# A hybrid decoder layer on one core: fewer vector steps, v's transpose in full products, gate rank in 16-bit halves, low rank products' low half with zeros, bonus sums beside the next key norm

## The chip, the cores and the metric

The kernel runs on one core of one Trainium2 chip. The metric is the device time of one execution in microseconds, the median over several runs. Engines are named as the profile names them: PE is TensorE (matrix products; PEld its loads of the stationary block), DVE is VectorE, ACT is ScalarE, POOL is GpSimd, and SP issues the DMAs. A matrix product `matmul(ps, lhsT, rhs)` holds `lhsT` stationary in the array and streams `rhs` through it; a product with fewer than 128 rows or columns uses a part of the array, and products on different parts can run at the same time. "64*128" in a profile row is such a part: 64 rows, 128 columns.

## The reference

The model is one layer over 4096 tokens of width 1024. Two head groups read the same normalised input, and one projection follows their gated outputs.

```python
h = _rmsnorm(x, norm_w);  u = (h @ w_in)
# gated linear attention: 4 heads, key 64, value 128, gate rank 16
log_a = log_sigmoid(glr @ gate_up + gate_bias) / 16
o = gla_chunked(q, k, v, log_a);  o = o * rsqrt(mean(o*o) + eps) * gla_norm_w
gla_out = o * silu(gg)
# RWKV-7: 8 heads of 64; mixed = shifted token mix of r, rk, rv, wl, al
w = -softplus(-(w0 + tanh(wl) @ w_up)) - 0.5;  decay = exp(-exp(w))
a = sigmoid(a0 + al @ a_up)
kk = normalise(rk * k_k);  rk = rk * (1 + (a - 1) * k_a)
y = rwkv7_scan(r, decay, rk, rv, kk, a)     # S = S(diag(w) - kk^T(a kk)) + v^T k;  y = S r
y = (y - mean(y)) * rsqrt(var(y) + eps) * ln_w + ln_b
bonus = sum(r * rk * r_k) * rv
rwkv_out = (y + bonus) * silu(rg)
out = rmsnorm(x + concat(gla_out, rwkv_out) @ w_out)
```

## The kernel before, in words

Features lie on the 128 partitions and tokens along the free dimension. The tokens are taken in 8 blocks of 512 (`TB`); the recurrent parts work in chunks of 64 tokens for RWKV (`C`, 8 chunks a block) and 128 for the gated attention. A **unit** is one block of one pair of RWKV heads: 4 pairs x 8 blocks = 32 units, numbered u. Two heads of 64 fill the 128 partitions; `lo` and `hi` are their halves.

The large projections are done in 16-bit halves: weights and inputs are split into a high and a low float16 part, and three products (high-high, high-low, low-high) are summed. These are the rows `bank<-x,wr`, `bank<-x,wg`, `bank<-x,wo` and `bank<-wg,x`. The small stages use 32-bit products, of which the profile counts two instructions each.

The work is written as generators, the streams: `stream_x` (input and its norm), `stream_w` (splitting the weights, once, and the setup), `stream_a` (per unit `rwkv_ab`: projections, decay, key norm, the products inside a chunk, the triangular inverse, v), `stream_i` (`rwkv_i`: joins the 32x32 inverses into 64x64 ones), `stream_c` (`rwkv_c`: the chain over the chunks, spawning `rwkv_d`, the group norm, bonus and gate), `stream_p` and `stream_g` (the gated attention) and `stream_o` (output projection). While they run, nothing is issued: each operation is recorded with a cost from `cost` (line 312) and its dependencies. Then `forward` and `backward` (line 234 on) plan the order of all instructions on every engine, as a list plan by how late each may start, and the instructions are issued in that order. So all instructions carry line 368, and groups are told apart by tile names. A changed operation, or a changed cost, lets the plan set another order anywhere.

What the change touches:

- `newton` (620) computes a reciprocal square root of 128x128 sums on VectorE: a first guess by integer arithmetic (a shift into `nt`, then a subtraction into `ny`) and two iterations. It serves the key norm (`a`), the group norm of RWKV (`c`) and the other norms (`g`).
- `stat_mm` (637) sums over the features of each head with four products on column groups of the array; `bcast` (641) writes the rows to DRAM and reads them back broadcast, three DMAs on SP.
- `lora_mm` (772) computes decay and a from rank 64: a product of 128 rows with `uh` (high part, against the high and low halves of the input) and one of 64 rows with `ul` (low part).
- `rwkv_ab` (780): `rn` is the key norm; at the end of a unit the bonus sums are made from `r`, which by then holds r·rk·r_k: `stat_mm(pst, bones, r)`, a copy to `brow`, `bcast`, and a product with v into `bv`. Then v is transposed into `sv`, 16 products of 64x64 with `c64`, which also takes the mean over the head from v. `De`, `Do`, `Nb` (`de`, `do`, `nb`) hold the operands of two units in turn; unit u writes them when the chain of unit u-2 is done.
- `rwkv_i` (911): `Ta` is a transpose, `Vs` the copied first product, and a second product gives the missing block of the inverse.
- `rwkv_c` (935): per chunk a product into `ch`, a copy to `us`, a product, two copies to `sv`, a product, and a scaled sum with `psd` on VectorE gives the next state. `y` collects the output.
- `rwkv_d` (977): square, sums, root, broadcast, then the affine norm, the gate `tg` and the maximum for the 16-bit split.
- `gla_lr` (1002) and `gla_pair` (1061): the gate's 16 features, in four partial sums, and the gate itself.
- `setup` (1266): prepares gate and low rank weights once, early in the run.

## Time and profile before

| | |
|---|---|
| median of 3 runs | 2419.3 us (2418.5 to 2422.08) |
| the profiled execution | 2425.58 us, span 2423.8 us |
| TensorE busy | 2301.9 us, 95% of the span |
| VectorE busy | 1691.6 us, 70% |
| ScalarE busy | 1219.0 us, 50% |
| GpSimd busy | 851.4 us, 35% |
| TensorE clock granted, mean | 0.982 |
| instructions | 54428 |

In a group's row, "x64 | 18.2, 386 | 0.0" means 64 instructions, 18.2 us of busy time together, 386 ns from start to end of one, and no idle time before them; since products overlap, the time that one of them costs is the distance to the next start, which the timeline shows. A timeline row is start, length, engine, operation, out<-in, array part, shape, count, and in brackets the idle time ahead of it with what ended that. A row of waits is: who waited, for whom, us in total, how often, the longest. The table of stretches has for each the busy time of every engine, the granted clock, and the DMA share.

### The profile page before, as it was taken

The page shows a single profiled execution, that of the slowest core. Times are in us where ns is not written, and L with a number is a line of the kernel's source. Part 1 is how long each engine was busy: PE and PEld are TensorE (multiplying, and loading weights), DVE is VectorE, ACT ScalarE, POOL GpSimd, SP SyncE. Part 2 cuts the span into 40 slices and gives each one's busy share as a digit, 9 for nine tenths or more (in the row PEclk, how much of TensorE's full clock was granted, in tenths as well). Part 3 has the DMA queues.
Part 4 walks back from the last instruction along what each step waited for, and adds up shares of the span by engine and source line. Part 5 has one row for each costly group of instructions (what it writes and reads, how often), then busy time and mean ns, then how long its engine had stood idle before and what let it go on. Part 6 is the DMA issues. An engine that isn't in the chain of part 4 may idle for free.

```text
span 2423.8 us, 54428 instructions
## 1 busy us (share of the span) xinstructions
PE 2301.9 (95%) x20710; PEld 1344.5 (55%) x20710; DVE 1691.6 (70%) x3866; ACT 1219.0 (50%) x3123; POOL 851.4 (35%) x2217
## 2 busy tenths in 40 slices
PE   7899999999999999999999999999999998999986
PEld 3555565455555656545564555645565564654643
DVE  7877877568675776676675687666867577666755
ACT  7576565455454555444644545455445455534342
POOL 4442234434323533315334243343334353331300
PEclk9898999999999999999999999999999999999987
DMA  6675545355334543455424553345533454344431
GB/s 196 205 229 184 160 145 172 110 170 151 95 102 129 169 126 97 112 145 168 112 80 122 171 151 103 98 124 162 151 94 98 130 182 116 104 109 116 137 91 58
DMA packets 275387, 325.54 MB, mean 134 GB/s; under 512 B 131652, under 2 KB 132788, under 8 KB 275124
## 3 DMA queue, kind: packets, MB, share of 16 engines
q1 hardware_dynamic: 275124, 322.06, 46.0%
q8 instruction: 162, 2.65, 0.5%
q14 instruction: 101, 0.83, 0.1%
HBM read 276.90 MB, written 45.05 MB: 133 GB/s over the span
## 4 chain that ended last, share of the span: by engine, by line
PE 63%; DVE 22%; DMA 6%; ACT 5%; issue 2%; SPq 1%; POOL 1%; DVEq 0%; ACTq 0%; POOLq 0%
PE bank L368 56%; PE ch L368 6%; DVE nta L368 2%; PE y L368 2%; DVE bk L368 2%; DVE Nb L368 2%; DVE De L368 1%; DVE Do L368 1%; DVE mgg L368 1%; DVE mgr L368 1%; DMA bv<-bcdb 1%; DVE gbc L368 1%; SPq L368 1%; DVE cy L368 1%; DVE sv L368 1%
## 5 line engine op out<-in xcount | busy, mean ns | idle before, releaser
L368 PE MATMUL bank<-x,wr 128*128 128x512 f16 x3264 | 811.3, 382 | 13.2 <-DVE De L368 5.7
L368 POOL TENSOR_TENSOR tm<-Tc,f 128x60 f32<-128x60 f32 (+24 forms) x961 | 338.5, 352 | 661.7 <-DMA f<-nd 405.5
L368 PEld LDWEIGHTS <-wr 128*128 128x128 f16 x3264 | 309.1, 100 | 319.2 <-issue 32.4
L368 PE MATMUL bank<-x,wg 128*128 128x512 f16 x1536 | 388.8, 380 | 5.4 <-DMA wg<-wdr 4.4
L368 POOL TENSOR_TENSOR Tc<-Tc,tm 128x60 f32<-128x60 f32 (+24 forms) x961 | 342.3, 356 | 73.2
L368 PE MATMUL bank<-x,wo 128*128 128x512 f16 x1488 | 364.0, 385 | 0.7 <-DVE nva L368 0.5
L368 DVE SCALAR_TENSOR_TENSOR sv<-ch,PC,psd 64x64 f32<-64x64 f32 x448 | 126.2, 282 | 214.5 <-PE ch L368 205.9
L368 POOL TENSOR_TENSOR xacc<-xacc,xr 128x512 f32<-128x512 f32 x98 | 131.8, 1345 | 374.0 <-ACT xr L368 211.5
L368 ACT ACTIVATE psd<-sv,PC 64x64 f32<-64x64 f32 x512 | 171.6, 342 | 122.3 <-DVE sv L368 115.4
L368 PEld LDWEIGHTS <-wg 128*128 128x128 f16 x1536 | 143.8, 99 | 152.1 <-issue 9.6
L368 PEld LDWEIGHTS <-wo 128*128 128x128 f16 x1488 | 143.0, 101 | 143.4 <-issue 9.3
L368 PEld LDWEIGHTS <-x 128*128 128x128 f16 x3120 | 189.8, 99 | 33.1 <-issue 13.4
L368 PE MATMUL bank<-wg,x 128*128 128x128 f16 x3072 | 206.2, 220 | 1.7 <-DMA wg<-wdr 1.7
L368 ACT COPY sv<-ch 64x64 f32<-64x64 f32 x512 | 104.6, 204 | 100.2 <-PE ch L368 93.1
L368 ACT ACTIVATE sa<-bank,mu_s 128x512 f32<-128x512 f32 x104 | 71.5, 687 | 137.0 <-PE bank L368 135.7
L368 POOL MEMSET Tc<- 32x8 f32 (+1 forms) x160 | 23.6, 148 | 318.2 <-DMA td<-Tc 303.5
L368 PEld LDWEIGHTS ch<-us,Nb 128*128 128x128 f32 x512 | 87.2, 191 | 57.2 <-ACT us L368 42.7
L368 ACT COPY us<-ch 128x64 f32<-128x64 f32 x256 | 53.3, 208 | 125.0 <-PE ch L368 122.4
L368 PEld LDWEIGHTS ch<-sv,bk 128*128 128x128 f32 x512 | 89.4, 191 | 48.1 <-ACT sv L368 32.7
L368 PE MATMUL ch<-sv,bk 128*128 128x128 f32 x512 | 106.8, 291 | 5.6 <-ACT sv L368 5.6
L368 PE MATMUL ch<-us,Nb 128*128 128x64 f32 x512 | 95.6, 269 | 11.5 <-ACT us L368 9.1
L368 PEld LDWEIGHTS ch<-sv,De 128*64 128x64 f32 x512 | 49.3, 135 | 98.9 <-issue 42.6
(327 smaller groups left out, 4115.4 us busy)
## 6 DMA issues: line engine op xcount, KB each, us to landing
wr<-wdr SPq DMA_DIRECT2D x256, 256.0 KB
wg<-wdr SPq DMA_DIRECT2D x184, 256.0 KB
xr<-in_xT_dram SPq DMA_DIRECT2D x176, 256.0 KB
wo<-wdr SPq DMA_DIRECT2D x128, 256.0 KB
f<-nd SPq DMA_DIRECT2D x128, 128.0 KB
x<-in_wt_dram SPq DMA_DIRECT2D x29, 512.0 KB
wdr<-wo SPq DMA_DIRECT2D x25, 512.0 KB
out_dram<-mgg SPq DMA_DIRECT2D x33, 256.0 KB
```

The costliest lines, as they stand in the source:

```text
L368: put(t0, self.name, d, lag, cols, tiles, tab, outs, ins, lambda: f(*a, **kw))
```

## The change

- `newton`: the shift and the subtraction become one step, a product with -0.5 and a sum on the integer view.
- `lora_mm`: `ul` becomes two tiles of 128 rows, of which the other 64 are zero; the low product now uses all 128 rows.
- The bonus sums of a unit with p = 0, 1 or 2 are put down in a list and made in the next unit, in the second quarter of the bank of that unit's key norm sums; its copy, broadcast and product with v follow the key norm's broadcast. A unit with p = 3 does them itself, where they stood. `rwkv_d` waits until the unit's bonus has been recorded. The copy to `brow` now also applies the gate's scale.
- The affine step of `rwkv_d` with its scale is folded into the neighbouring steps (`lnh`, made at setup).
- v's transpose: 4 products of 128x128x128 with a block diagonal `c64` and 4 copies, instead of 16 products and 2 copies.
- `rwkv_i`: the first product writes 64 rows, with 32 that are not used, and one copy takes all 128.
- `rwkv_c`: one `psd` step over both heads and both halves instead of two; `us` and `psd` have one buffer instead of two; the square of y is taken from the accumulator before the copy.
- The gate: the 16 features are computed twice, side by side (`wgs` columns 16 to 31); one copy becomes the float16 high part and the other the low part, and the 16-row weights are laid out as two float16 tiles. Two 16-bit products take the place of one 32-bit product.
- `cost` gets other values for some vector operations.

```diff
@@ cost
+            if op == "copy_predicated":
+                runs = 0.09
+            elif n == 256 and o.shape[0] != 128:
+                runs += 0.04 if op == "transpose" else 0.09
+            elif op == "tensor_scalar" and few > 1:
+                runs = 0.06
@@ newton
-        V.tensor_scalar(t.bitcast(I32), v.bitcast(I32), 1, None, ALU.logical_shift_right)
-        V.tensor_scalar(y.bitcast(I32), t.bitcast(I32), -1.0, float(0x5F1FFFF9), ALU.mult, ALU.add)
+        V.tensor_scalar(y.bitcast(I32), v.bitcast(I32), -0.5, float(0x5F1FFFF9), ALU.mult, ALU.add)
@@ lora_mm
-        q = slice(64 * i, 64 * i + 64)
         T.matmul(ps, lhsT=uh[i][:, cs_], rhs=LR[0][i], start=True, stop=False)
-        T.matmul(ps, lhsT=ul[q, cs_], rhs=LR[0][i][q], start=False, stop=True)
+        T.matmul(ps, lhsT=ul[i][:, cs_], rhs=LR[0][i], start=False, stop=True)
@@ rwkv_ab
         pst = yield from need("r")
         stat_mm(pst, bones, rn)
+        late = bonus.pop() if bonus else None
+        if late:
+            stat_mm(pst[:, P:2 * P], bones, late[1])
         bcast(newton(pst[:, 0:P], None, None, 1e-24, "a"), 2, rn, "a")
+        if late:
+            add_bonus(pst[:, P:2 * P], *late)
...
-        yield after(r)
-        pst = yield from need("r")
-        stat_mm(pst, bones, r)
-        brow = sb(rt, [P, P], F32, "brow", 1)
-        S.copy(brow, pst[:, 0:P])
         bv = tA("bv", 2)
-        bcast(brow, 2, bv, "b")
-        V.tensor_tensor(bv, bv, v, ALU.mult)
-        rel("r")
+        bonus.append((u, r, v, bv, hinv[:, i:i + 1]))
+        if p == 3:
+            yield after(r)
+            pst = yield from need("r")
+            stat_mm(pst, bones, r)
+            add_bonus(pst[:, 0:P], *bonus.pop())
+            rel("r")
...
-        for c in range(NC):
-            t_ = slice(C * c, C * c + C)
-            T.matmul(pv[64:128, c, :], lhsT=v[0:64, t_], rhs=c64[0:64, :], start=True, stop=True)
-            T.matmul(pv[0:64, c, :], lhsT=v[64:128, t_], rhs=c64[64:128, :], start=True, stop=True)
-        S.copy(sv[64:128, :, 0, :], pv[64:128])
-        S.copy(sv[0:64, :, 1, :], pv[0:64])
+        for c in range(4):
+            T.matmul(pv[:, c], lhsT=v[:, P * c:P * c + P], rhs=c64, start=True, stop=True)
+        for k, q in enumerate((lo, hi)):
+            for e, o in enumerate((hi, lo)):
+                S.copy(sv[o, k::2, e, :], pv[q, :, e, :])
+    def add_bonus(rows, u, r, v, bv, iv):
+        brow = sb(rt, [P, P], F32, "brow", 1)
+        S.activation(brow, rows, AF.Copy, scale=iv)
+        bcast(brow, 2, bv, "b")
+        V.tensor_tensor(bv, bv, v, ALU.mult)
+        bonuses.add(u)
@@ rwkv_i
-                T.matmul(pl[q0 + 32:q0 + 64, 0, c, :], lhsT=nb[q0:q0 + 32, c, q0 + 32:q0 + 64], rhs=Ta[q0:q0 + 32, c, :],
+                T.matmul(pl[q0:q0 + 64, 0, c, :], lhsT=nb[q0:q0 + 32, c, q0:q0 + 64], rhs=Ta[q0:q0 + 32, c, :],
                          start=True, stop=True)
-        for q0 in (0, 64):
-            V.tensor_copy(Vs[q0 + 32:q0 + 64], pl[q0 + 32:q0 + 64, 0])
+        V.tensor_copy(Vs, pl[:, 0])
@@ rwkv_c
-            us = sb(rt, [P, 64], F32, "us", 2)
+            us = sb(rt, [P, 64], F32, "us")
-            psd = sb(rt, [P, 64], F32, "psd", 2)
-            for q_, d_, e in dd:
-                S.activation(psd[q_], sv[q_, c, e, :], AF.Copy, scale=PC[q_, c])
+            psd = sb(rt, [P, 2, 64], F32, "psd")
+            S.activation(psd, sv[:, c], AF.Copy, scale=PC[:, c])
...
+        S.activation(rs, py.rearrange("p c t -> p (c t)"), AF.Square)
         S.copy(y, py.rearrange("p c t -> p (c t)"))
-        S.activation(rs, y, AF.Square)
@@ rwkv_d
-        V.scalar_tensor_tensor(y, y, pkt[:, PK_LW + p:PK_LW + p + 1], bv, ALU.mult, ALU.add)
-        V.tensor_scalar(y, y, pkt[:, PK_LB + p:PK_LB + p + 1], hinv[:, i:i + 1], ALU.add, ALU.mult)
+        V.scalar_tensor_tensor(y, y, lnh[:, p:p + 1], bv, ALU.mult, ALU.add)
-        V.tensor_tensor(mgt[4 + p], y, tg, ALU.mult)
+        V.scalar_tensor_tensor(mgt[4 + p], y, lnh[:, 4 + p:5 + p], tg, ALU.add, ALU.mult)
@@ gla_lr
-        glr = sb(rt, [P, TB], F32, "glr")
-        S.activation(glr, pr, AF.Copy, scale=invs[:, NWT:NWT + 1])
+        glr = sb(rt, [P, TB], F16, "glr")
+        S.activation(glr, pr, AF.Copy, scale=1.0 / GUP)
+        S.activation(glr, glr, AF.Copy, scale=gus[:, 2:3])
+        V.scalar_tensor_tensor(glr, pr, 1.0 / GUP, glr, ALU.mult, ALU.add)
@@ gla_pair
-        T.matmul(pz, lhsT=gupt[:, P * j:P * j + P], rhs=glr, start=True, stop=True)
+        for i in range(2):
+            T.matmul(pz, lhsT=guw[:, i, P * j:P * j + P], rhs=glr, start=i == 0, stop=i == 1)
@@ setup
-        G.memset(wgs, 0.0)
         split(raw, scl[:, NWT:NWT + 1], wgs[:, 0, :, 0:16], wgs[:, 1, :, 0:16])
-        G.memset(gupt, 0.0)
-        for g in range(4):
-            D.dma_start(gupt[32 * g:32 * g + 16, :], gup)
+        G.tensor_copy(wgs[:, :, :, 16:32], wgs[:, :, :, 0:16])
+        gr = sb(rt, [P, 1024], F32, "f4", 1)[:, 0:256]
+        for g in range(8):
+            D.dma_start(gr[16 * g:16 * g + 16], gup)
...
+        yield from absmax_scale(gr, gus[:, 3:4], gus[:, 4:5], "W")
+        S.activation(guw[:, 0], gr, AF.Copy, scale=gus[:, 3:4])
+        V.scalar_tensor_tensor(guw[:, 1], gr, gus[:, 3:4], guw[:, 0], ALU.mult, ALU.subtract)
+        V.tensor_scalar_mul(guw[:, 1], guw[:, 1], gus[:, 1:2])
...
-        D.dma_start(c64, ck[:, CK_C64:CK_C64 + 64])
+        for q in (slice(0, 64), slice(64, 128)):
+            D.dma_start(c64[q, q], ck[q, CK_C64:CK_C64 + 64])
```

More of the change, by code (lines that the diff above doesn't have):

```diff
@@ L47 @@
 NC = TB // C
+GUP = 2.0 ** 19
 DECAY = math.exp(-0.5)
@@ L453, in hymba_kernel @@
     uh = [sb(one, [P, 512], F16, f"uh{i}") for i in range(2)]
-    ul = sb(one, [P, 512], F16, "ul")
+    ul = [sb(one, [P, 512], F16, f"ul{i}") for i in range(2)]
+    for t in ul:
+        G.memset(t, 0.0)
     usc = sb(one, [P, 8], F32, "usc")
-    gupt = sb(one, [P, 256], F32, "gupt")
+    guw = sb(one, [P, 2, 256], F16, "guw")
+    gus = sb(one, [P, 8], F32, "gus")
+    gbz = sb(one, [P, 2], F32, "gbz")
     half_p = sb(one, [P, 12], F32, "half_p")
@@ L579, in split_w @@
                 V.tensor_tensor(gnh[:, h:h + 1], hinv[:, i:i + 1], pkt[:, PK_GN:PK_GN + 1], ALU.mult)
+            else:
+                for j in range(i - W_RG, 8, 4):
+                    V.tensor_tensor(lnh[:, j:j + 1], hinv[:, i:i + 1], pkt[:, PK_LW + j:PK_LW + j + 1], ALU.mult)
         if n < ND:
@@ L977, in rwkv_d @@
     def rwkv_d(p, b, mgt, y, rs, bv, tg):
+        u = 4 * b + p
+        if u not in bonuses:
+            yield lambda: u in bonuses
         yield after(rs)
```

32 lines of the change are left out of this document (21 added, 11 removed).

## The prediction

> **What bounds the kernel now.** I read the page's first two parts and its chain, then who TensorE waits for, then busy time by stretch.
>
> ```profile
> span 2423.8 us, 54428 instructions
> PE 2301.9 (95%) x20710; PEld 1344.5 (55%) x20710; DVE 1691.6 (70%) x3866; ACT 1219.0 (50%) x3123; POOL 851.4 (35%) x2217
> PE 63%; DVE 22%; DMA 6%; ACT 5%; issue 2%; SPq 1%; POOL 1%; DVEq 0%; ACTq 0%; POOLq 0%
> ```
>
> ```profile
> PE bank L368 <- DVE bk L368: 15.5, 10, 6.0
> PE ch L368 <- DVE sv L368: 9.7, 17, 2.9
> ```
>
> ```profile
> core 0: us, PE busy (x) PEld busy (x) DVE busy (x) ACT busy (x) POOL busy (x), PEclk, DMA share, GB/s
> 0.00:30.00 30.00, 15.64 (x95) 7.53 (x96) 20.65 (x70) 18.03 (x28) 15.39 (x34) 1.00 0.75 239
> 200.00:2200.00 2000.00, 1944.23 (x17784) 1139.19 (x17784) 1384.16 (x3057) 1002.49 (x2635) 744.18 (x1965) 0.99 0.46 131
> 2350.00:2400.00 50.00, 39.85 (x286) 21.50 (x283) 27.61 (x72) 14.87 (x48) 0.00 (x0) 0.91 0.22 64
> ```
>
> TensorE is the bound: it idles 2423.8 - 2301.9 = 122 us, and only 2000 - 1944 = 56 us of that lie in the long middle. The rest is the start and the tail. No one waits much: the worst releaser costs 15.5 us. So an edit is worth what it takes from TensorE's own time, and an edit on VectorE or ScalarE only what it takes from those 122 us. I therefore price TensorE first, by start-to-next-start in the timeline, because matmul durations overlap.
>
> **v's transpose.** 16 products 64x64 a unit (two instructions each) become 4 of 128x128x128, 8 instructions.
>
> ```profile
> 1166.16 1.15 PE L368 MATMUL bank<-c,v 64*64 64x64 f32 x32
> 1167.24 0.49 PE L368 MATMUL ch<-sv,bk 128*128 128x128 f32 x2
> ...
> 1148.95 1.05 PE L368 MATMUL bank<-SC,vt 128*128 128x128 f32 x8
> 1149.84 0.59 PE L368 MATMUL bank<-x,wr 128*128 128x512 f16 x2
> ```
>
> Old: 1167.24 - 1166.16 = 1.08 us. New: eight instructions of exactly the new shape take 1149.84 - 1148.95 = 0.89 us. So 0.19 saved, and another 0.10 for the change of array form (next fence) where the old group stood alone between full products, which the timeline shows for 10 of 32 units: 32 x 0.19 + 10 x 0.10 = 7.1 us. Bounds: 0 (the new group pays an entry of its own) to 9.
>
> A rule speaks against this edit and the next. The Trainium skill, page "TensorEngine Tiling (Array Packing)", section "Theoretical Speedup", gives tiling up to 2x where a dimension is 64 or less, which is what both edits give up; by that rule this edit would double its 1.08 us, adding 35 us over 32 units. The rows above contradict it for 32-bit products: 0.89 against 1.08.
>
> **Low half of the low rank products.** 64 products go from 64 to 128 rows.
>
> ```profile
> 1027.28 0.38 PE L368 MATMUL bank<-lr,uh 128*128 128x512 f16 x1
> 1027.59 0.39 PE L368 MATMUL bank<-lr,ul 64*128 64x512 f16 x1
> 1027.91 0.39 PE L368 MATMUL bank<-x,wg 128*128 128x512 f16 x1
> ...
> 1189.11 0.39 PE L368 MATMUL bank<-lr,ul 64*128 64x512 f16 x2
> 1189.42 0.27 PE L368 MATMUL ch<-sv,De 128*64 128x64 f32 x1
> ...
> 715.95 2.12 PE L368 MATMUL bank<-x,wr 128*128 128x512 f16 x9
> 717.90 0.27 PE L368 MATMUL ch<-sv,bk 128*128 128x128 f32 x1
> ```
>
> A full product in a stream takes 1.95/9 = 0.217 us. The lone 64-row one takes 0.31 us before it starts and 0.32 until the next, so each form change costs 0.10 us: 0.42 against 0.217. But two that follow each other share the array: 0.31 us for the pair at 1189.11, against 0.43 in full form. The timeline has 30 single and 17 pairs; 18 singles and 5 pairs stand alone. 18 x 0.20 + 12 x 0.10 - 12 x 0.11 - 5 x 0.02 = 3.4 us saved. Bounds: 0 to 7.
>
> **Gate rank.** One 32-bit product becomes two 16-bit ones, 16 times.
>
> ```profile
> 1064.20 1.02 PE L368 MATMUL bank<-glr,gupt 128*128 128x512 f32 x2
> 1065.06 0.39 PE L368 MATMUL ch<-sv,bk 128*128 128x128 f32 x2
> ```
>
> 0.86 us against 2 x 0.217: 16 x 0.43 = 6.9 us saved, bounds 6 to 8. It adds per block one ScalarE pass and one VectorE pass over 128x512 (0.59 and 0.76 us by the cy and bv rows of the last fence); the gate's tile is only needed in a later stage, and TensorE has other projections until then. Without that cover it is 8 x 1.35 = 11 us.
>
> **Bonus sums** go beside the next key norm in 24 of 32 units.
>
> ```profile
> 1165.80 0.42 PE L368 MATMUL bank<-r,bones 128*32 128x128 f32 x8
> ...
> 1042.12 0.43 PE L368 MATMUL bank<-rn,bones 128*32 128x128 f32 x8
> 1042.37 0.40 PE L368 MATMUL bank<-crs,bones 128*32 128x128 f32 x8
> ...
> 1189.81 0.43 PE L368 MATMUL bank<-rn,bones 128*32 128x128 f32 x8
> ...
> 1267.58 0.43 PE L368 MATMUL bank<-crs,bones 128*32 128x128 f32 x8
> ```
>
> Alone it takes 1166.16 - 1165.80 = 0.36 us (plus 0.10 where it stands between full products); right behind another sum of the same form the next one starts after 0.25. So 0.16 on the mean: 24 x 0.16 = 3.8 us, bounds 2 to 6. The move carries a ScalarE copy, one DMA out, two broadcast DMAs on SP and a VectorE product past the inverse's gathers and the weight loads on SP. For unit 15 it moves from 1165.8 to 1189.8, and its user (the product after the norm at 1267.6) comes 78 us later, so it costs nothing. Without that cover the VectorE product would wait in order for its broadcast: 28.8 us of such waits stand in the profile already (last fence).
>
> **The inverse's first product** writes 64 rows instead of 32, so the stationary block has 64 columns.
>
> ```profile
> 1055.81 0.69 PE L368 MATMUL bank<-Ta,Nb 32*32 32x32 f32 x32
> 1056.43 3.41 PE L368 MATMUL bank<-x,wo 128*128 128x512 f16 x15
> ...
> 1004.12 0.33 PE L368 MATMUL ch<-us,Nb 128*128 128x64 f32 x2
> 1004.28 1.24 PE L368 MATMUL bank<-x,wo 128*128 128x512 f16 x5
> ...
> 1009.08 0.22 PE L368 MATMUL y<-De,sv 128*64 128x64 f32 x1
> 1009.14 0.22 PE L368 MATMUL y<-De,sv 128*64 128x64 f32 x1
> ```
>
> Now 0.62 us. The streamed columns stay 32, so it could stay at 0.62 (lower bound, 0). But a block wider than what is streamed is not free: us times Nb, 128 stationary and 64 streamed columns, takes 0.16 us for two instructions, where 64 and 64 repeat after 0.06. If the second waits for its load, 0.16 - 0.06 = 0.10 us load 128 columns, 0.053 load 64; on two row tiles at once that is 0.027 an instruction, 32 x 0.027 + 0.10 = 0.96 us. The nearest upper row is v's 64x64 group, 1.08. I take 0.97, since the load row matches the new ratio of two to one: +0.35 x 32 = **+11 us**, bounds 0 to 15.
>
> The Trainium skill, page "TensorE: Matmul & The Clock Gate", section "LDWEIGHTS (loading the stationary operand)", says the load takes columns/1.2 ns whatever the rows; 64 columns would be an estimated 53 ns, the same as from the row here.
>
> **VectorE and ScalarE.**
>
> ```profile
> L368 DVE TENSOR_SCALAR nta<-nva 128x128 int32<-128x128 int32 x96 | 25.8, 269 | 1.9
> L368 DVE TENSOR_SCALAR cy<-cy,pkt,hinv 128x512 f32<-128x512 f32 x32 | 17.4, 543 | 0.6
> L368 DVE COPY Vs<-bank 32x256 f32<-32x256 f32 x64 | 27.1, 423 | 8.4 <-PE bank L368 7.3
> L368 DVE TENSOR_TENSOR bv<-bv,v 128x512 f32<-128x512 f32 x32 | 24.4, 762 | 29.0 <-DMA bv<-bcdb 28.8
> L368 ACT ACTIVATE psd<-sv,PC 64x64 f32<-64x64 f32 x512 | 171.6, 342 | 122.3 <-DVE sv L368 115.4
> L368 ACT ACTIVATE Gst<-gt,nm 128x128 f32<-128x128 f32 x16 | 6.4, 399 | 3.4 <-DVE gt L368 3.1
> L368 ACT COPY cy<-y 128x512 f32<-128x512 f32 x32 | 18.7, 585 | 49.3 <-PE y L368 49.1
> ```
>
> Gone are the shift of the square root (25.8), the second affine step of the RWKV output (17.4) and half the copies of Vs (13.5); added about 10 (the gate, the setup). VectorE loses some 46 us. On ScalarE 512 pieces of 0.342 become 256 of about 0.40 (the 128x128 row): -69 us, with some +15 for four copies of v instead of two, the gate and the scaled bonus row. That is 3% and 4% of these engines. I value it by the idle time it can shorten: of the middle's 56 us I take an eighth, -7, bounds 0 to -25. The single buffers of us and psd cost nothing: each next one needs a state that is written after the last reader of the old.
>
> In the tail nothing covers these steps, so they count in full: one step of two roots (0.27 each), the affine step 0.54, and the copy of y, behind which the square no longer waits, 0.59 less some 0.1 for reading the accumulator: -1.6. The square holds that accumulator about 0.7 us longer; the next state chain starts some 10 us after, which hides it. At the start the setup gains a maximum, its four scale steps, and two weight halves: some 10 small steps in line (0.15 to 0.4 us each), 2 to 4 us, while TensorE has other projections; I take +2, bounds 0 to +6.
>
> **Sum**: -7.1 - 3.4 - 6.9 - 3.8 + 11 = -10.2 on TensorE; -7 - 1.6 + 2 = -6.6 of idle time: -17. The profiled execution took 2425.6 us (span 2423.8 and 1.8 around it), 6.3 above the median of the runs, 2419.3. So 2408.6 profiled, **2402** as a median, 0.7% faster. A measurement tells 0.2%, 4.8 us, from no change.
>
> **The rivals.** *A, the wide block is free* (0.62 stays): for it, the streamed columns are unchanged and 32x32 repeats after 0.017 an instruction; against it, the us row. 2402 - 11 = 2391; with VectorE's idle bound 2375. *B, waits don't follow*: each unit's inverse passes through DMAs and POOL before its state chain, which nothing here shortens; TensorE then waits for what it filled before, and half the TensorE gain goes with all of the idle gain: 2419 - 5 + 2 = 2416, no measurable change. For it: after the first wait row, TensorE waits for bk and De, which that loop feeds. Against it: the loop contains the state chain, which gets shorter too. *C, slower: the wide block's two row tiles do not load side by side.* Then 32 x 0.053 + 0.10 = 1.80 us against 0.62, +38 us over 32 units instead of +11: 2429. It decides against the change from +28 us, that is from 1.5 us a group. For it: a 64-column block spans both halves' column tiles, which no row shows with 32 rows. Against it: the 64x64 rows, 1.08 for 32, do overlap.
>
> **How the numbers follow.** Forecast 0.55, A 0.18, B 0.15, C 0.12. Forecast's own range 2390 to 2412. Faster: 0.55 + 0.18 and a third of B's spread, 0.05, = 0.78; no change 0.11 (B's rest, some of C's low end); slower 0.11. The range that holds 8 in 10 leaves out C's upper and A's lower part: 2380 to 2422.
>
> **What would show it.** In the timeline after: v's products as 8 instructions in about 0.89 us; no 64-row product with ul; the gate's pair in 0.43; the bonus sum 0.25 behind a key norm; the group writing from Ta at 0.97 (0.62 would be A, 1.8 C). TensorE's busy sum should fall by about 10 us and its idle by 7; VectorE to about 1645, ScalarE to about 1165. I am wrong if busy falls and idle grows by as much (B), or if TensorE's busy rises.

## The result

The changed kernel takes 2381.3 us (median of four runs, 2378.8 to 2382.2) against 2419.6 us for the kernel before beside it: a ratio of 0.984, 95% interval 0.982 to 0.986, so 38 us or 1.6% faster. The forecast was 2402 us, 0.7% faster. The sign was right and the time lies inside the range of 2380 to 2422, at its very edge, but below the forecast's own 2390 to 2412; the gain is 2.2 times the one forecast, and rival B's and C's times, 2416 and 2429, are clearly missed. Rival A's, 2391 down to 2375, bracket the time, but not by A's cause, as the rows below show.

### The profile page after: what moved, and what is told of

The parts are those of the page before. It is cut to its first block, busy times and chain, and to the rows that moved or that the text cites. A ratio compares the mean times of both kernels' runs of the same rounds, so it can differ in the third digit from the quotient of the medians.

```text
span 2377.1 us, 52750 instructions
## 1 busy us (share of the span) xinstructions
PE 2276.7 (96%) x19944; PEld 1350.5 (57%) x19944; DVE 1659.1 (70%) x3737; ACT 1158.3 (49%) x2940; POOL 870.0 (37%) x2219
## 5 line engine op out<-in xcount | busy, mean ns | idle before, releaser
L375 POOL TENSOR_TENSOR Tc<-Tc,tm 128x60 f32<-128x60 f32 (+24 forms) x961 | 359.9, 375 | 74.0
L375 PE MATMUL bank<-wg,x 128*128 128x128 f16 x3072 | 200.6, 221 | 5.1 <-DMA wg<-wdr 5.1
L375 ACT ACTIVATE psd<-sv,PC 128x128 f32<-128x128 f32 x256 | 102.2, 399 | 192.4 <-DVE sv L375 166.3
```

Source lines behind the costliest of these rows:

```text
L375: put(t0, self.name, d, lag, cols, tiles, tab, outs, ins, lambda: f(*a, **kw))
```

## The profile after, beside the one before

The first two lines of the page of the kernel after:

```profile
span 2377.1 us, 52750 instructions
PE 2276.7 (96%) x19944; PEld 1350.5 (57%) x19944; DVE 1659.1 (70%) x3737; ACT 1158.3 (49%) x2940; POOL 870.0 (37%) x2219
```

The span fell by 46.7 us (the profiled execution of before was one of its slower ones, 6.3 us above the median, so this is 8 more than the medians tell). TensorE is busy 25.2 us less and idle 2377.1 - 2276.7 = 100.4 us instead of 121.9: 21.5 less, where 6.6 were forecast. VectorE lost 32 us, ScalarE 61.

To see where, busy time by stage: start, middle, end. The columns are those of the table by stretch in the prediction (the stretch, its length, busy time of PE, PEld, DVE, ACT and POOL, the granted clock, DMA). First the kernel before, whose middle is shown there:

```profile
0.00:200.00 200.00, 166.94 (x1264) 95.67 (x1264) 157.85 (x443) 132.90 (x260) 80.60 (x183) 0.95 0.68 210
2200.00:2423.80 223.80, 190.69 (x1665) 109.65 (x1662) 149.54 (x369) 83.62 (x230) 26.59 (x69) 0.90 0.35 99
```

The same of the kernel after:

```profile
0.00:200.00 200.00, 163.56 (x1142) 91.15 (x1144) 152.69 (x439) 127.77 (x247) 82.70 (x180) 0.94 0.65 205
200.00:2200.00 2000.00, 1956.41 (x17402) 1164.94 (x17404) 1385.65 (x2992) 964.95 (x2513) 762.03 (x1972) 0.99 0.46 133
2200.00:2377.10 177.10, 156.72 (x1404) 94.44 (x1404) 120.74 (x307) 65.60 (x182) 25.28 (x67) 0.95 0.36 108
```

TensorE's idle time by stage, length less busy: start 33.1 to 36.4 us (+3.4; +2 forecast), middle 55.8 to 43.6 (-12.2; -7 forecast), end 33.1 to 20.4 (-12.7; -1.6 forecast). And the clock: the end was run at 0.90 of full speed before and at 0.95 after. I call (1 - granted clock) x length the time lost to the clock, an upper bound of it since an idle TensorE loses nothing. At the end it goes from 223.8 x 0.10 = 22 us to 177.1 x 0.05 = 9. Over the whole span, with the mean granted clock of 0.982 before and 0.986 after, it is 43.6 and 33.3: 10 us that the prediction did not price at all. What is left of the busy time, TensorE's work at full clock, went from 2301.9 - 43.6 = 2258 to 2276.7 - 33.3 = 2243: -15, where -10.2 was forecast. So **the 46.7 us are 15 of work, 10 of clock and 21.5 of idle time.** Counted only over the time in which TensorE is busy, the clock loss is 31.1 us before and 23.1 after, and the split reads 17, 8 and 21.5.

At the end the last units of RWKV come sooner after each other. The sums for the norm of units 30 and 31 on TensorE, before and then after, from the timeline (start, duration, instruction):

```profile
2352.42 0.43 PE L368 MATMUL bank<-crs,bones 128*32 128x128 f32 x8
2386.10 0.42 PE L368 MATMUL bank<-crs,bones 128*32 128x128 f32 x8
```

```profile
2322.88 0.43 PE L375 MATMUL bank<-crs,bones 128*32 128x128 f32 x8
2342.65 0.43 PE L375 MATMUL bank<-crs,bones 128*32 128x128 f32 x8
```

Unit 31 follows unit 30 after 33.7 us before and 19.8 after, and behind it remain 38 and 34 us. So of the 46.7 us, 29.5 had been won by unit 30, 13.9 are won between the two units and 3.3 behind them.

**The terms on TensorE.** The timeline of after, stand-alone groups and what follows them:

```profile
150.88 1.05 PE L375 MATMUL bank<-c,v 128*128 128x128 f32 x8
151.77 4.48 PE L375 MATMUL bank<-x,wg 128*128 128x512 f16 x20
...
249.42 0.43 PE L375 MATMUL bank<-rn,bones 128*32 128x128 f32 x8
249.67 0.40 PE L375 MATMUL bank<-r,bones 128*32 128x128 f32 x8
...
280.30 0.59 PE L375 MATMUL bank<-glr,guw 128*128 128x512 f16 x2
280.73 1.24 PE L375 MATMUL bank<-x,wg 128*128 128x512 f16 x5
...
291.18 1.12 PE L375 MATMUL bank<-Ta,Nb 32*64 32x32 f32 x32
292.24 1.04 PE L375 MATMUL bank<-x,wg 128*128 128x512 f16 x4
```

By start to next start: v's transpose 0.89 us (0.89 forecast), a bonus sum 0.25 behind a key norm (0.25), the gate's pair 0.43 (0.43), the inverse's wide product 1.06 (0.97; 0.62 before). Summed over all their rows of the timeline, less idle time before the next: v's transpose 35.6 to 31.7 us (-3.9), the two halves of the low rank products 30.5 to 28.7 (-1.8), the gate 14.6 to 7.3 (-7.3), bonus and key norm sums 22.9 to 19.4 (-3.5), the wide product 21.9 to 36.2 (+14.3). The group rows of the two profiles agree on the two largest:

```profile
L368 PE MATMUL bank<-Ta,Nb 32*32 32x32 f32 x1024 | 24.2, 194 | 2.7 <-DVE De L368 1.4 <-DVE Ta L368 1.3
L368 PE MATMUL bank<-glr,gupt 128*128 128x512 f32 x32 | 16.9, 610 | 0.4 <-DVE mgr L368 0.3 <-ACT glr L368 0.2
```

```profile
L375 PE MATMUL bank<-Ta,Nb 32*64 32x32 f32 x1024 | 38.8, 221 | 2.5 <-DVE Ta L375 2.5
L375 PE MATMUL bank<-glr,guw 128*128 128x512 f16 x32 | 9.7, 379 | 0.6 <-ACT ta L375 0.4 <-DVE glr L375 0.2
```

These terms make -2 alone, so most of the 15 us does not lie in the changed groups' own rows. One place that fits are the rows next to them: the array changes its form 1049 times instead of 1207, and at the 0.10 us that the prediction read for a change, 158 fewer would be up to 16 us. This is an estimate; no run isolates it. The work of one and the same set of TensorE instructions also moves with their order: in the nine kernels below that have the 20710 of before it lies between 2252 and 2266 us.

**The start.** The maximum of the second low rank matrix on VectorE, and the key norm sum of the first unit, before and after:

```profile
26.91 0.69 DVE L368 TENSOR_REDUCE amW<-glr 128x1 f32<-128x512 f32 x1
44.82 0.42 PE L368 MATMUL bank<-rn,bones 128*32 128x128 f32 x8
```

```profile
39.42 0.68 DVE L375 TENSOR_REDUCE amW<-rgs 128x1 f32<-128x512 f32 x1
53.50 0.43 PE L375 MATMUL bank<-rn,bones 128*32 128x128 f32 x8
```

The gate's preparation stands ahead of that matrix and delays it by 12.5 us and the first unit by 8.7. TensorE's idle time grew by only 3.4 there, since it had projections to do.

## The experiments

Two theories were put against each other. **Matrix theory**, that of the prediction: TensorE is the bound, an edit is worth what it takes from TensorE, and VectorE and ScalarE steps are worth a small share. **Vector theory**: TensorE's work is laid around chains of small VectorE and ScalarE steps; shorter chains shrink idle time and raise the clock, while matrix work alone is mostly turned into waiting. A third suspect came up on the way: the order of instructions is written by a planner, and any edit makes it write another order. In the expectations the matrix theory is called W, the vector theory L, and the planner's order P; in those of the two direct loads, L is the narrower claim that a loop over two units sets the pace.

All medians are in us; the ratio is to the kernel before on the same chip. Idle, clock loss and work are as defined above, for the profiled execution.

| kernel | median | ratio (95%) | idle: start, middle, end | clock loss | work |
|---|---|---|---|---|---|
| before | 2419.6 | 1 | 33, 56, 33 | 44 | 2258 |
| p1_before, p1b_before (other order) | 2430.4, 2423.3 | 1.003 (1.001-1.006), 1.001 (1.000-1.002) | 34, 62, 30; 36, 53, 32 | 46, 39 | 2256, 2262 |
| e1_cost | 2413.0 | 0.996 (0.994-0.997) | 36, 47, 27 | 39 | 2263 |
| e3_pe, e3b_pe | 2439.3, 2420.2 | 1.007 (1.005-1.008), 1.000 (0.999-1.001) | 38, 69, 31; 37, 63, 27 | 51, 36 | 2244, 2251 |
| e10_ch | 2404.7 | 0.992 (0.991-0.994) | 32, 58, 25 | 22 | 2266 |
| e13_dve | 2400.5 | 0.991 (0.990-0.993) | 35, 46, 25 | 38 | 2253 |
| e2_vec, p3_vec | 2381.5, 2401.8 | 0.983 (0.982-0.985), 0.991 (0.989-0.994) | 34, 47, 23; 32, 45, 28 | 21, 34 | 2252, 2256 |
| after, p2_after | 2381.3, 2382.0 | 0.984 (0.982-0.986), 0.984 (0.982-0.986) | 36, 44, 20; 36, 42, 20 | 33, 31 | 2243, 2250 |
| e17_oldvec | 2416.4 | 0.997 (0.995-0.998) | 40, 51, 28 | 41 | 2254 |
| e18_oldch | 2392.5 | 0.987 (0.985-0.990) | 35, 41, 24 | 41 | 2250 |
| e4_narrow | 2394.0 | 0.988 (0.987-0.990) | 37, 60, 21 | 38 | 2236 |
| e14_, e14b_, e14c_lategate | 2390.1, 2381.4, 2388.4 | 0.986 (0.985-0.988), 0.984 (0.982-0.986), 0.986 (0.984-0.988) | 36, 38, 24; 37, 41, 23; 35, 43, 23 | 48, 43, 36 | 2242, 2238, 2250 |
| d1_pool | 2425.0 | 1.001 (1.000-1.002) | 34, 60, 34 | 36 | 2260 |
| d2_pe | 2477.4 | 1.022 (1.020-1.024) | 31, 36, 31 | 37 | 2342 |

### The vector edits alone

Before, with the square root's start in one step, the affine step folded into its neighbours, the psd piece in one step (us and psd with one buffer each), and the square ahead of the copy of y; TensorE's products are those of before.

```diff
-        V.tensor_scalar(t.bitcast(I32), v.bitcast(I32), 1, None, ALU.logical_shift_right)
-        V.tensor_scalar(y.bitcast(I32), t.bitcast(I32), -1.0, float(0x5F1FFFF9), ALU.mult, ALU.add)
+        V.tensor_scalar(y.bitcast(I32), v.bitcast(I32), -0.5, float(0x5F1FFFF9), ALU.mult, ALU.add)
...
-            for q_, d_, e in dd:
-                S.activation(psd[q_], sv[q_, c, e, :], AF.Copy, scale=PC[q_, c])
+            S.activation(psd, sv[:, c], AF.Copy, scale=PC[:, c])
...
-        V.tensor_scalar(y, y, pkt[:, PK_LB + p:PK_LB + p + 1], hinv[:, i:i + 1], ALU.add, ALU.mult)
```

> Kernel before with the vector and scalar edits alone (one step of the root fewer, the affine step folded, one psd step, the square ahead of the copy); all matrix products as before, old planner costs. Theory W as I had it on record: -9 us, 2411, TensorE busy unchanged. Theory L (TensorE's idle time hangs on the vector and scalar chain more than an eighth): 2400 or less, TensorE's idle time from 122 to 102 or less.

Measured: 2381.5, ratio 0.983. In this order these edits alone give as much as the whole change; in a second order, below, half of it. The page of this kernel, and its middle and end by stretch:

```profile
span 2378.3 us, 54229 instructions
PE 2273.8 (96%) x20710; PEld 1329.8 (56%) x20710; DVE 1659.3 (70%) x3746; ACT 1144.8 (48%) x2867; POOL 867.8 (36%) x2217
```

```profile
200.00:2200.00 2000.00, 1953.19 (x18002) 1143.69 (x18004) 1382.05 (x3002) 951.87 (x2444) 758.66 (x1967) 1.00 0.47 133
2200.00:2378.30 178.30, 155.04 (x1456) 92.16 (x1452) 121.47 (x311) 64.03 (x176) 25.51 (x67) 0.96 0.36 104
```

TensorE executes the same 20710 instructions as before and is busy 28 us less: up to 22 of that is the clock loss by the definition above (mean granted clock 0.991 against 0.982), 17 if it is counted over busy time alone. Its idle time is 104.5 instead of 121.9, and the end looks like that of the kernel after. This goes against the matrix theory's price: the prediction gave VectorE and ScalarE together 8.6 us.

### The matrix edits alone

Before, with v's transpose in full products, the low half with zeros, the gate in two halves and the bonus sums beside the next key norm (the wide product is not in it).

```diff
-        for c in range(NC):
-            t_ = slice(C * c, C * c + C)
-            T.matmul(pv[64:128, c, :], lhsT=v[0:64, t_], rhs=c64[0:64, :], start=True, stop=True)
-            T.matmul(pv[0:64, c, :], lhsT=v[64:128, t_], rhs=c64[64:128, :], start=True, stop=True)
+        for c in range(4):
+            T.matmul(pv[:, c], lhsT=v[:, P * c:P * c + P], rhs=c64, start=True, stop=True)
...
-        T.matmul(ps, lhsT=ul[q, cs_], rhs=LR[0][i][q], start=False, stop=True)
+        T.matmul(ps, lhsT=ul[i][:, cs_], rhs=LR[0][i], start=False, stop=True)
...
-        T.matmul(pz, lhsT=gupt[:, P * j:P * j + P], rhs=glr, start=True, stop=True)
+        for i in range(2):
+            T.matmul(pz, lhsT=guw[:, i, P * j:P * j + P], rhs=glr, start=i == 0, stop=i == 1)
...
+        bonus.append((u, r, v, bv, hinv[:, i:i + 1]))
```

> Kernel before with four matrix edits alone (v's transpose in full products, low rank zeros, 16-bit gate, bonus beside the key norm); the inverse's first product, vector steps and planner costs as before. Theory W: -21 us, 2398, all of it from TensorE's busy time. Theory L: the products saved turn into waits, 2410 or more, idle time up by 10 us. If changes of array form weigh more than I counted (50 fewer groups in part form after the change instead of 39, and the granted clock up from 0.982): 2390 or less.

Measured: 2439.3, ratio 1.007: slower. The page, the middle, and the first two rows of who TensorE waits for (total us, times, longest):

```profile
span 2434.1 us, 53062 instructions
PE 2295.1 (94%) x19944; PEld 1343.9 (55%) x19944; DVE 1701.2 (70%) x3889; ACT 1232.6 (51%) x3196; POOL 872.1 (36%) x2219
```

```profile
200.00:2200.00 2000.00, 1930.56 (x17076) 1138.12 (x17074) 1396.01 (x3075) 1015.31 (x2700) 753.65 (x1962) 0.99 0.45 130
```

```profile
PE ch L369 <- ACT us L369: 16.6, 26, 2.0
PE ch L369 <- ACT sv L369: 12.2, 19, 2.5
```

Work fell by 14 us, to 2244, and idle time grew by 17, to 139, of it 13.6 in the middle; the clock took 7.5 more. That is the outcome that rival B named, for these edits: what TensorE saves comes back as waiting. The cause is another: the waits that lead the list are those of the state chain for ScalarE, not those of B's loop, and ScalarE has 14 us more to do here (four copies of v for two, the gate). Whether the saving itself or this added work makes the waits, no run separates. In the kernel before they were:

```profile
PE ch L368 <- ACT us L368: 9.1, 19, 1.8
PE ch L368 <- ACT sv L368: 5.6, 10, 0.8
```

The same kernel in another order (a planning allowance, below, of 0.06 for 0.05):

> The four matrix edits alone, second draw (0.06); the first gave 2439 with TensorE's work at full clock 14 us less, idle time 17 more, and the key norm of unit 0 at 57 instead of 45. If the matrix edits alone never pay on this kernel: 2425 or more again. If 2439 was a poor draw: 2400 to 2415.

Measured: 2420.2, ratio 1.000; work 2251, idle time 128. So the slowdown of the first order isn't the edits' own; that they win nothing alone holds in both.

### Parts of the vector edits

ScalarE's part alone (psd in one step, single buffers of us and psd, in the kernel before):

```diff
-            us = sb(rt, [P, 64], F32, "us", 2)
+            us = sb(rt, [P, 64], F32, "us")
-            psd = sb(rt, [P, 64], F32, "psd", 2)
-            for q_, d_, e in dd:
-                S.activation(psd[q_], sv[q_, c, e, :], AF.Copy, scale=PC[q_, c])
+            psd = sb(rt, [P, 2, 64], F32, "psd")
+            S.activation(psd, sv[:, c], AF.Copy, scale=PC[:, c])
```

> Kernel before with only the chain's psd step changed (one 128x128 step of ScalarE in place of two 64x64, single buffers); everything else and the planner's costs as before. Before: 2419.6 to 2423.8 in the comparisons so far; the vector edits together gave -42. Theory L (the state chain's own length, 256 steps, sets the pace): ScalarE's two pieces of 0.34 us stood between the copy of us and the copies of sv, so 0.15 to 0.3 us a chunk go, with 256 chunks -25 to -45 in all: 2385 or less. Theory W: -5, 2416.

Measured: 2404.7, -17 us on the same chip. The rest of them (square root, affine step, square ahead of the copy; psd as before):

```diff
-        V.tensor_scalar(t.bitcast(I32), v.bitcast(I32), 1, None, ALU.logical_shift_right)
...
-        V.tensor_scalar(y, y, pkt[:, PK_LB + p:PK_LB + p + 1], hinv[:, i:i + 1], ALU.add, ALU.mult)
...
+        S.activation(rs, py.rearrange("p c t -> p (c t)"), AF.Square)
-        S.activation(rs, y, AF.Square)
```

> Kernel before with the edits on VectorE's steps and the square alone (root, affine step, square ahead of the copy), ScalarE's psd in two pieces as before. Draws of the kernel before lie at 2421 to 2430, the psd step alone at 2405, all vector edits at 2381 and 2402. If VectorE's relief carries the larger part: 2400 or less, idle time 110 or less. If psd carries it: 2415 or more.

Measured: 2400.5, -21 us. All of the vector edits together gave -42 in their first order and -21 in the second (below), so the parts need not add up. They do it differently: the second lowers the middle's idle time from 56 to 46, the first leaves it at 58 and shows less clock loss.

### The same steps put back into the changed kernel

The square root's two starting steps and the affine step come back; all else is the kernel after.

```diff
-        V.tensor_scalar(y.bitcast(I32), v.bitcast(I32), -0.5, float(0x5F1FFFF9), ALU.mult, ALU.add)
+        V.tensor_scalar(t.bitcast(I32), v.bitcast(I32), 1, None, ALU.logical_shift_right)
+        V.tensor_scalar(y.bitcast(I32), t.bitcast(I32), -1.0, float(0x5F1FFFF9), ALU.mult, ALU.add)
...
+        V.tensor_scalar(y, y, pkt[:, PK_LB + p:PK_LB + p + 1], hinv[:, i:i + 1], ALU.add, ALU.mult)
```

> The changed kernel with the root's two steps and the output's affine step put back (about 43 us of VectorE's time); all matrix edits, psd and the rest as changed. Draws of the changed kernel: 2381 and 2382. If VectorE's steps set TensorE's idle and half-clock time (alone on the kernel before they gave -21): 2395 to 2405. If the matrix edits carry the gain here: 2381 to 2388.

Measured: 2416.4, ratio 0.997. That is 6 us faster than before on the same chip, where the kernel after is 38 faster: some 32 us are gone, although every matrix edit, the new costs of the planner and the psd step are still in. The page:

```profile
span 2413.4 us, 52933 instructions
PE 2294.9 (95%) x19944; PEld 1352.8 (56%) x19944; DVE 1697.4 (70%) x3857; ACT 1154.1 (48%) x2940; POOL 863.6 (36%) x2219
```

VectorE has 38 us more to do than in the kernel after, and the span of the profiled execution is 36 longer: 18 of it idle time, 8 clock, 10 work. On an engine that is busy 70% of the span these steps were worth nearly their full duration in this order, where the prediction took an eighth of one stage's idle time for them. It was run in one order only; the largest move by order alone, below, is 20 us.

The psd step put back into two pieces, with two buffers of us and psd, again in the kernel after:

```diff
-            S.activation(psd, sv[:, c], AF.Copy, scale=PC[:, c])
+            for q_, d_, e in dd:
+                S.activation(psd[q_], sv[q_, c, e, :], AF.Copy, scale=PC[q_, c])
```

> The changed kernel with only the chain's psd back in two pieces of 64x64. If ScalarE's pieces in the chain matter as on the kernel before (-17): 2393 to 2403. If not: 2381 to 2388.

Measured: 2392.5, ratio 0.987: 30 us faster than before on the same chip instead of 38, so some 9 us are gone, about the size of the scatter between orders. The idle time stays at 100; clock loss takes 7 and work 6.

### The order alone

The planner's allowance after the state chain's steps, 0.05 us, is set to 0.06 or 0.04. No instruction changes, only the order that comes out.

```diff
-XL = 0.05
+XL = 0.06
```

> Kernel before with a planning allowance inside the state chain of 0.06 us instead of 0.05: the same instructions, almost every one at another place in its engine's order. It measures how far a new plan alone moves the time. Theory P (the excess over my sum is the plan): 10 us or more away from 2421, either way. Theory L (the vector edits themselves): within 6 us.

> The same with 0.04 us: a second draw of the plan for the kernel before. Theory P: 10 us or more from 2421 or from the draw with 0.06. Theory L: within 6 us.

> The changed kernel with 0.06 us in place of 0.05: a second draw of its plan. Theory P: back toward what the sum gives, 2395 or more. Theory L: 2381 +-6.

> The vector edits alone (2381.5 in the run before) with 0.06 us in place of 0.05. Theory P: 2395 or more, since 2381.5 was a good draw. Theory L: 2381 +-6.

Measured: the kernel before 2430.4 and 2423.3 beside its own 2422.4; after 2382.0; the vector edits 2401.8 beside their 2381.5. So one and the same set of instructions moves by up to 20 us with the order that the planner happens to write. A difference of some 10 us between two kernels of one order each is no proof of an edit. The vector edits (-42 and -21) and the matrix edits (+16 and -1, each against before on its chip) stay apart in every pairing. The planner's new cost values alone, in the kernel before:

```diff
+            if op == "copy_predicated":
+                runs = 0.09
+            elif n == 256 and o.shape[0] != 128:
+                runs += 0.04 if op == "transpose" else 0.09
+            elif op == "tensor_scalar" and few > 1:
+                runs = 0.06
```

> Kernel before with the planner's new cost values alone: every instruction the same, only their order new. Theory W (the gain is work taken from TensorE plus idle time cut by shorter vector steps): within 6 us of 2419.6, TensorE busy 2302 +-5. Theory P (the gain beyond my sum is a luckier plan): 2405 or less, with idle time of TensorE down by 10 us or more.

Measured: 2413.0, -11 us, about the size of this scatter. Whether better costs give a better order or this is chance stays open. The prediction had no term for them.

### The wide product of the inverse

The kernel after with the first product writing 32 rows again and two copies of Vs:

```diff
-                T.matmul(pl[q0:q0 + 64, 0, c, :], lhsT=nb[q0:q0 + 32, c, q0:q0 + 64], rhs=Ta[q0:q0 + 32, c, :],
+                T.matmul(pl[q0 + 32:q0 + 64, 0, c, :], lhsT=nb[q0:q0 + 32, c, q0 + 32:q0 + 64], rhs=Ta[q0:q0 + 32, c, :],
-        V.tensor_copy(Vs, pl[:, 0])
+        for q0 in (0, 64):
+            V.tensor_copy(Vs[q0 + 32:q0 + 64], pl[q0 + 32:q0 + 64, 0])
```

> The changed kernel with only the inverse's first product put back to 32 rows and its two copies. Theory W: TensorE's busy time falls by about 14 us (the group from 1.05 to 0.62 us, 32 times), VectorE's grows by 13: 2381 - 12 = 2369, better than both. Theory L: the second copy in the chain of each unit costs as much as the product saves: 2378 to 2385.

Measured: 2394.0, ratio 0.988: 30 us faster than before on the same chip instead of 38, so some 9 us worse than the kernel after. The work is 2236, 22 less than before, where the prediction's terms without the wide product add up to -21.2. This one order agrees, but the two orders of the matrix edits alone, with the same TensorE instructions, gave -14 and -7. And the middle is idle for 60 us instead of 44. One wide copy in place of two (27.1 us in the prediction's row) gives VectorE 13.7 us back, by its row of after:

```profile
L375 DVE COPY Vs<-bank 128x256 f32<-128x256 f32 x32 | 13.4, 419 | 18.5 <-PE bank L375 18.5
```

Here that outweighs 14 us more of TensorE. With one order of the narrow product, 9 us is within the scatter, so the sign of this part is not settled.

### What paces the kernel: two direct loads

Ten more memsets of 0.32 us on POOL ahead of the inverse of each unit of the kernel before, 101 us in all; their result is overwritten.

```diff
+        for _ in range(10):
+            G.memset(tm, 0.0)
```

> Kernel before with ten extra memsets of a scratch tile on POOL in every unit, ahead of the inverse's steps: about 3 us more in the path from a unit's inner products to its chain, no work for TensorE. Theory L (a loop over two units, inner products, inverse on POOL, chain, paces the kernel): up to 16 x 3 = 48 us slower, at least +20. Theory W (TensorE's work is the bound, other projections fill): +5 or less.

The group of them in the profile, and the ten of unit 12 in POOL's timeline, with the first multiplication of that unit's inverse as the last row:

```profile
L368 POOL MEMSET tm<- 128x256 f32 x320 | 101.0, 316 | 17.7
```

```profile
897.91 3.80 POOL L368 MEMSET tm<- 128x256 f32 x10
910.46 0.90 POOL L368 MEMSET Tc<- 128x256 f32 x5 [8.76 <-DMA td<-Tc]
942.78 0.24 POOL L368 TENSOR_TENSOR tm<-Tc,f 128x31 f32<-128x31 f32 x1 [31.42 <-DMA f<-nd]
```

Measured: 2425.0, ratio 1.001 (1.000 to 1.002): 101 us more of POOL's time cost at most 0.2%, 5 us. But the run does not test the loop that rival B reasoned by. In every one of the 32 units POOL sits idle for at least 10 us between the last of the ten memsets and the inverse's first multiplication, mostly until the unit's data `f` has arrived by DMA; so the memsets filled time in which POOL waited and made the path from a unit's inner products to its chain no longer. Whether that loop paces the kernel stays open. In the kernel before, the state chain's first product with the inverse starts within 1 us of the last copy into the inverse in 26 of 32 units, so no slack shows at that place.

Fourteen more full products per unit on TensorE, whose result no one reads:

```diff
+        for n in range(14):
+            T.matmul(px, lhsT=uh[0][:, cs_], rhs=LR[0][0], start=True, stop=True)
```

> Kernel before with 14 extra full 16-bit products in every unit (3.0 us of TensorE by the 0.217 us of one), into a bank that nobody reads. Theory W: 32 x 3.0 = 97 us slower less what fills idle time, +75 to +100. Theory L alone (loop paces, TensorE has room): +30 or less. Both near bound: between.

```profile
span 2477.0 us, 55356 instructions
PE 2379.2 (96%) x21158; PEld 1379.4 (56%) x21158; DVE 1689.6 (68%) x3866; ACT 1226.0 (49%) x3123; POOL 855.3 (35%) x2217
```

Measured: 2477.4, +56 us. By 0.217 us a product they should take 14 x 32 x 0.217 = 97; work grew by 84, and idle time fell by 24 and clock loss by 6. TensorE's own work counts, but only two thirds of it show in the time: the added products fill gaps. If the same share holds the other way round, an estimate, 15 us of work taken away are worth some 10.

### The gate's preparation behind the low rank matrices

The kernel after, with the gate's setup moved behind the low rank setup, and the gate waiting for its own flag:

```diff
+                yield from setup_gate()
+                done["SG"] = 1
...
+        if not done["SG"]:
+            yield lambda: done["SG"]
```

> The changed kernel with the gate's preparation moved behind the preparation of the low rank weights (same instructions; gla_lr waits for it). In the traces the key norm of unit 0 starts at 54 us in the changed kernel, 45 in the one before, and the scale of the second low rank matrix is found at 39.4 instead of 26.9, behind the gate's. If this start loss carries to the end: 2381 - 8 = 2373 or less, key norm of unit 0 back at 48 or before. If the start is hidden by other projections, as I had it on record: 2378 to 2385.

> The changed kernel with the gate's preparation behind the low rank weights, second draw (0.06). The first draw was 22 us ahead of the changed kernel at the sums of unit 30 (2301 against 2323) and lost all of it in unit 31 (46 us from one to the next against 20). If that loss is the plan's end alone: 2365 +-8. If the earlier start is always paid back at the end: 2381 or more.

> The same, third draw (0.04): 2365 +-8 if the first draw's end was the plan's, 2381 or more if the earlier start is always paid back.

Measured: 2390.1, and with the other two allowances 2381.4 and 2388.4. The norm sums of units 30 and 31 in the first of them:

```profile
2301.40 0.43 PE L375 MATMUL bank<-crs,bones 128*32 128x128 f32 x8
2347.25 0.43 PE L375 MATMUL bank<-crs,bones 128*32 128x128 f32 x8
```

The first unit starts at 45 us again and unit 30 is 21 us ahead of the kernel after, but unit 31 is 5 us behind it. What the start gains is lost at the end, and the late start of the changed kernel costs nothing that shows. None of the versions run beats the kernel after.

## Why the prediction was right and wrong

**Right: sign, and TensorE's work.** The work fell by 15 us (by 7 to 18 if any of the two orders of after is set against any of the three of before), against 10.2. On the mean, the nine kernels with the TensorE instructions of before have 2258 us of work and the seven with those of after 2247: 12 less. The durations read from rows of before for v's transpose, the gate and the bonus came out to the hundredth. Term by term they are less exact: v's transpose gave 3.9 in its own rows, not 7.1, because many groups are cut in two by other products or stand behind a part of the array. The four savings together came to 16.5 us in their own rows, and to 15 in the mean work of the three kernels that have them without the wide product, where 21.2 were forecast. That the sum fits as well as it does is in part luck.

**The wide product: 1.06 us, not 0.97.** +14.3 us instead of +11, inside the bounds of 0 and 15. Rival A (free, 0.62) and rival C (1.80) are both refuted by the row. The estimate from the load of 128 columns, read off us times Nb, was in the right place: (1.06 - 0.10) / 16 = 0.060 us for each pair of instructions on the two row tiles, against 0.053. But half of the 0.10 us that the prediction reads for 128 columns is 0.05, not 0.053; with 0.05 its sum would give 0.90 for the group. The Trainium skill's page "TensorE: Matmul & The Clock Gate", section "LDWEIGHTS (loading the stationary operand)", gives columns/1.2 ns, an estimated 53 ns for 64 columns; the row has 60.

**Wrong: "I value it by the idle time it can shorten: of the middle's 56 us I take an eighth, -7".** This is the step that failed, and with it the tail's -1.6. TensorE's idle time was to fall by 6.6 us in all and fell by 21.5. The middle's fell by 12, more than the 7 but within the bounds of 0 to -25; the end's fell by 12.7. The -1.6 priced only what follows the last unit, where 3.3 us of the span were won; that the last units would come closer together, 13.9 us, had no term. The sentence that led there, "an edit is worth what it takes from TensorE's own time", took the high busy share for a proof that the other engines are covered. The added products show that it is two thirds true; the VectorE steps put back show what it misses, some 32 us for 38 us of steps. Across all kernels run, those with the square root and affine edits have 98 to 106 us of idle time (119 with the narrow product, which adds VectorE copies), those without 111 to 139, with the matrix edits or without them (98 only where 84 us of products were added to fill the gaps). VectorE's own time fell by 32 us where 46 were forecast, but with the same steps it moves between 1689 and 1710 us by order alone. The reading that the next state chain starts some 10 us after the square, which was to hide the longer hold of the accumulator, was wrong too: in the trace of before the chain starts between 1.5 us ahead of the square's end and 42 us after it, in 9 of 31 units within 1.3 us. What the longer hold cost, no run separates.

**Missing: the clock.** The quoted row of the last stretch showed 0.91, but the prediction took TensorE's busy time as work. It contained up to 43.6 us of clock loss (31.1 over busy time), and 10 of them (8) went, net all at the end, where TensorE runs with gaps. How the gaps lie counts for more than their sum. In the clock records of the twenty profiles the clock is either full or half, in stretches of 3.4 us or a multiple. In the 3.4 us ahead of a half-clock stretch TensorE was busy for 40% of the time on the mean, ahead of a full-clock step for 98%. The kernel with psd alone idles 116 us in all and loses at most 22; the first kernel with the late gate idles 98 and loses up to 48.

**No row names the wait.** No single releaser accounts for the idle time that went. The largest waits before, for bk (15.5) and sv (9.7), are smaller after:

```profile
PE ch L375 <- DVE sv L375: 6.4, 12, 1.6
PE ch L375 <- ACT us L375: 4.3, 10, 1.1
PE bank L375 <- DVE bk L375: 3.6, 3, 2.9
```

But with the vector edits alone bk stands first still, and that kernel is as fast:

```profile
PE bank L368 <- DVE bk L368: 12.4, 11, 3.2
```

The nearest to a common thread is the state chain: TensorE's waits for its sv and us add up to 24 to 27 us in three orders of before, 32 and 36 with the matrix edits alone, and 15 to 24 in after and the vector edits, two orders of each. Between the two profiles shown it is 9.5 of the 21.5 us. But the second order of after keeps 24 us of these waits and is as fast, so the chain is not shown to be where the gain lies. The rest is spread over many short waits, and I can't name it.

**Rival B** was right for the matrix edits by themselves and wrong for the change, because the change also shortens what TensorE waits for. Its reason, the loop over two units, was not tested: the memsets on POOL did not lengthen it. **The start** cost 3.4 of idle time against 2, inside the bounds; starting earlier, in the three orders with the late gate, brought nothing in the end.

**Open**: how the gain is divided between VectorE's and ScalarE's steps (21 and 17 alone, some 32 and 9 when put back); how far the loop through DMA and POOL paces the kernel; the shares of the planner's costs and of the wide product, both near the scatter of the order; and why one order of the same instructions is 20 us better than another.

## What to carry to other kernels

An engine at 95% busy is not proof that steps on a 70% engine are covered: where its work is laid around serial chains, taking steps out of the chains can be worth nearly their full duration, and matrix work saved alone can return as waiting. Split the span of the bounding engine into work, idle time and clock loss by stage, and price each; the end of a kernel, where work to fill gaps has run out, deserves its own line. When a load is added to test a path, look in the trace whether it ran on that path: the memsets here ran while their engine would have waited. And where a planner writes the order, run each version in two or three orders before a difference of half a per cent is given to an edit.

## What was not expected of the hardware

The same 20710 TensorE instructions took 2301.9 us of busy time in one kernel and 2273.8 in another that only has fewer vector steps, at granted clocks of 0.982 and 0.991. The clock halves behind some 3.4 us in which TensorE was mostly idle, so gaps that lie together cost more than the same gaps spread out. A product whose stationary block has 64 columns and whose streamed block has 32 repeats 1.7 times as slowly as with 32 and 32 (1.06 us against 0.62 for 32 instructions). And 4 full 32-bit products (128x128x128) take less time than the 16 quarter-size ones that do the same work, 0.89 against 1.08 us.
